# A running sum kept in HBM: ScalarE copies product blocks out of PSUM, an accumulating DMA adds them

## The chip, the cores and the metric

The kernel runs on one core of one Trainium2 chip. The core has TensorE (PE, with PEld for its weight loads), VectorE (DVE), ScalarE (ACT), GpSimd (POOL) and SyncE (SP), which work through queues of their own and wait for each other by semaphores. Tiles lie in SBUF or, as results of matmuls, in PSUM banks of 128 x 512 fp32; DMA engines move data between SBUF and HBM. The metric is the device time of one execution in microseconds, the median of the runs.

## The reference

One decoder layer for 1024 tokens of 1024 features, in fp32:

```python
x = LN1(ALPHA * x + 0.5 * swiglu(x, w_gate1, w_up1, w_down1))
x = LN2(ALPHA * x + mixer(x))
x = LN3(ALPHA * x + 0.5 * swiglu(x, w_gate2, w_up2, w_down2))
def swiglu(x, w_gate, w_up, w_down):
    return (silu(x @ w_gate) * (x @ w_up)) @ w_down
```

`D_FF` is 2816. The mixer (gated delta rule and gated linear attention) isn't touched by the change.

## The kernel before

*Tiles.* The tokens are 8 blocks of 128, in two halves of four. The features of a feed-forward layer are 22 blocks of 128. Every factor of a product is split into two parts hi and lo (`split`: ScalarE casts hi, VectorE subtracts to get lo), and a product is three matmuls. The layer's running sum is `acc`, eight SBUF tiles of 128 tokens x 1024, kept divided by ALPHA.

*A feature block.* `hidden` loads `w_gate` and `w_up` (each as two halves of 256 KB through the ring `wr` of 5, split into the ring `wh`/`wl` of 6), multiplies them with x (`proj`, 24 matmuls into a bank `pa`), and makes silu(gate) x up as tiles `gh`/`gl`. `down` multiplies with `w_down` (tiles `fh`/`fl`): for each token block and each half of the 1024 columns it runs `3 * len(hs)` matmuls into a bank `pd` (3 banks), and then one VectorE instruction adds the bank to `acc`:

```python
nc.vector.scalar_tensor_tensor(acc, p, scale / ALPHA, acc, ALU.mult, ALU.add, ...)
```

*Phases.* `run` has three parts. `ffn_groups(1, ...)` takes blocks 0 to 11 of the first layer, in six groups of two, each for all tokens: two `hidden` with both halves of the tokens, then 16 product blocks of six matmuls (8 token blocks x 2 column halves). `middle` does the rest of that layer for one half of the tokens at a time, the mixer, and the first 8 blocks of the second layer. `ffn_groups(2, ...)` takes blocks 8 to 17 in five groups of two, and then, as `last`, blocks 18 to 21 for each half together with the closing layer norm.

*What sets the order.* The code is written out in order, and a scheduler puts it into the queues. Each engine works in the order of its queue. SP issues all DMAs of the kernel before; a DMA that has to wait for a buffer holds up those behind it on SP. A ring's tile is written again only when the last reader of its earlier content is done. At the start, `acc` first serves as staging room for x transposed; `load_acc` then loads x into it.

Of the kernel before, what the change touches and what calls it, by code (L numbers as in the profile page):

```python
# [10 lines left out]
F32 = mybir.dt.float32  # L11
# [3 lines left out]
ALU = mybir.AluOpType  # L15
# [12 lines left out]
ALPHA = 2.0 ** 0.25  # L28
# the rows that the layer norms get here are the reference's over ALPHA
LN_EPS = 1e-5 / ALPHA ** 2  # L30
# [11 lines left out]
BANKS = {"pa": 2, "pd": 3, "pm": 3}  # L42
BUFS = {"w": 6, "h": 3, "xf": 3, "wr": 5, "f": 4, "g": 6, "raw": 1, "q": 1, "k": 2, "v": 1, "tt": 1, "z": 1, "on": 2, "am": 1, "pt": 1, "qd": 1, "vb": 1,
        "v0": 1, "v1": 1, "kd": 1, "mi": 1, "ui": 1, "wi": 2}
# [37 lines left out]
class Layer:  # L82
    def __init__(self, tc, ctx, a):
        self.tc, self.nc, self.a = tc, tc.nc, a
        pool = lambda name, bufs, **kw: ctx.enter_context(tc.tile_pool(name=name, bufs=bufs, **kw))
        self.cp = pool("cp", 1)
        self.xp = pool("xp", 1)
        self.wp = pool("wp", 1)
        self.sp = pool("sp", 1)
        self.ps = pool("ps", 1, space=PSUM)  # L90
        self.n = 0
        self.xh = [[None] * KB, [None] * KB]
        self.xl = [[None] * KB, [None] * KB]
        self.acc = [None] * KB
        self.mv = [None] * KB
        self.centred = {}

# [25 lines left out]
    def weight(self, src, pool=None, tag="w"):  # L123
        """The parts hi and lo of the two halves of the columns of src, in tiles of their own."""
        out = []
        for sl in HALVES:
            raw = self.u("wr", self.wp)
            self.nc.sync.dma_start(raw[:], src[:, sl])
            hi, lo = [self.wt(pool or self.wp, [HT], tag + t, BUFS[tag], F32R) for t in "hl"]
            self.split(hi[:], lo[:], raw[:])  # L130
            out.append((hi, lo))
        return out
# [28 lines left out]
    def load_x(self, half, k):  # L161
        h, l = self.xtile(half, k)
        c = 4 * half + k // 2
        if k % 2 == 0:
            # acc serves as staging room until it is loaded itself
            self.acc[c] = self.wt(self.xp, [D], f"acc{c}", 1)
        raw = self.acc[c][:, HALVES[k % 2]]
        self.nc.sync.dma_start(raw, self.a["xT"][half, k])
        self.split(h[:], l[:], raw)

    def load_acc(self, c):
        t = self.acc[c]
        self.tc.keep_in_program_order(self.nc.sync.dma_start(t[:], self.a["x"][c]))

# [13 lines left out]

    def down(self, hs, ws, half, scale, cs=range(4), sums=None, cuts=((0, HT), (HT, D)), ahead=1):
        """acc += scale / ALPHA * sum of h w for the half's token blocks cs; sums gets the new acc's sums over the columns."""  # L190
        nc = self.nc
        n = len(hs)
        units = [(c, d, cut) for d, cut in enumerate(cuts) for c in cs]
        while units:
            # the first few units take all but the last h first, which has just been computed
            now, units = units[:ahead], units[ahead:]
            ahead = 1
            yield 3 * n * len(now)
            ps = [self.bank("pd")[:, 0:cut[1] - cut[0]] for c, d, cut in now]
            for part in (range(n - 1), range(n - 1, n)) if len(now) > 1 else (range(n),):  # L200
                for p, (c, d, cut) in zip(ps, now):
                    sl, ds = slice(c * P, (c + 1) * P), slice(cut[0] % HT, (cut[1] - 1) % HT + 1)
                    for i in part:
                        (hh, hl), (wh, wl) = hs[i], ws[i][cut[0] // HT]
                        nc.tensor.matmul(p, hh[:, sl], wh[:, ds], start=(i == 0), stop=False)  # L205
                        nc.tensor.matmul(p, hh[:, sl], wl[:, ds], start=False, stop=False)  # L206
                        nc.tensor.matmul(p, hl[:, sl], wh[:, ds], start=False, stop=(i == n - 1))  # L207
            for p, (c, d, cut) in zip(ps, now):
                acc = self.acc[4 * half + c][:, slice(*cut)]
                nc.vector.scalar_tensor_tensor(acc, p, scale / ALPHA, acc, ALU.mult, ALU.add,  # L210
                                               accum_out=None if sums is None else sums[:, d:d + 1])
# [27 lines left out]
    def ln(self, i, half):  # L239
        """Normalises the half's acc, writes the parts hi and lo of the transpose of LN(acc)."""  # L240
        nc = self.nc
# [25 lines left out]
    def out_stats(self, c, sums):  # L267
        """The rows' means and reciprocal deviations; (acc - mean) * g in two temporary tiles."""
        nc = self.nc
# [54 lines left out]
    def hidden(self, idx, f, halves, pool, tags, bufs, tanh=False):  # L324
        """silu(x w_gate) * (x w_up) of one block of features (twice that with tanh), as parts hi and lo."""
        wgu = self.a[f"gu{idx}"]
# [30 lines left out]
    def ffn(self, idx, fs, half):  # L357
        """The blocks fs of features for one half of the tokens, two at a time."""
        for n in range(0, len(fs), 2):
# [7 lines left out]
    def ffn_groups(self, idx, groups, first=False, last=()):  # L367
        """Blocks of features in groups, both halves of the tokens, while the mixer needs no room."""
        with self.tc.tile_pool(name=self.nm("fx"), bufs=1) as fx:
            for n, fs in enumerate(groups):  # L370
                hs = []
# [6 lines left out]
                if first and n == 1:  # L378
                    self.load_constants()
            if last:  # L380
                for half in range(2):
                    hs = [now(self.hidden(idx, f, (half,), fx, ("gh", "gl"), BUFS["g"])) for f in last]
                    self.downs_group(idx, last, hs, (half,), fx, end=True)

    def downs_group(self, idx, fs, hs, halves, fx, first=False, end=False):
        ws = [self.weight(self.a[f"wd{idx}"][f], *((fx, "f") if 2 * n < BUFS["f"] else ())) for n, f in enumerate(fs)]
        if first:
            for c in range(KB):
                self.load_acc(c)
        for half in halves:  # L390
            for c in range(4):
                sums = self.tiny("sums", 2) if end and c < 3 else None
                last = end and half == 1 and c == 3
                work = self.down([h[half] for h in hs], ws, half, 0.5, [c], sums,
                                 ((0, HT), (HT, HT + HT // 2), (HT + HT // 2, D)) if last else ((0, HT), (HT, D)))
                if end:
# [28 lines left out]
    def misc(self, half):  # L425
        nc = self.nc
        sm = lambda tag, w=16: self.wt(self.sp, [w], tag, 1)
        # columns 64:128 repeat 0:64 in memory; here they become the parts lo, so the sum of both halves is the product
        w = []
# [77 lines left out]
    def finish(self, ons, half, blk, wz, wcol):  # L507
        """Gates heads' normalised outputs [token, dv] and adds their share of w_out."""
        nc = self.nc
# [17 lines left out]
    def pull(self, n, skip=0):  # L527
        """Emits about n products of the work that waits, from its entry number skip on."""
        while n > 0 and len(self.urgent) + len(self.filler) > skip:
# [30 lines left out]
    def gdn(self, h, half, free):  # L560
# [49 lines left out]

        # the inverse of each B0 x B0 diagonal block of I + A, column after column from the last
        m, w = self.u("mi"), self.u("wi")
# [7 lines left out]
        for j in range(B0 - 1, 0, -1):  # L620
            # row j of each block, in all of the block's partitions
            bk = self.wt(self.sp, [NC, B0], "bk", 2)
# [13 lines left out]
        for b in LEVELS:  # L636
            # the columns of the second halves of the blocks of 2 * b
            second = lambda a: a.rearrange("p (n t w) -> p n t w", t=2, w=b)[:, :, 1, :]
# [17 lines left out]
        for b in (32, 64):  # L656
            # block by block, as the halves of the blocks begin at partitions that the engines can start at
            blk = [(c, j, slice(j, j + b), slice(j + b, j + 2 * b)) for j in range(0, P, 2 * b) for c in C2]
# [4 lines left out]
            pw, m = self.bank("pm"), self.u("mi")  # L663
            # over all rows of the block, as the others are zero: all products that write a bank start at the same row
            for c, j, f, s in blk:
# [44 lines left out]
    def values(self, ws, half):  # L710
        """The pair's values with the tokens on the partitions: both weights have the columns of both heads, for half of the rows."""
        out = []
# [46 lines left out]
    def gla(self, p, half, free):  # L759
# [41 lines left out]
        for i, hb in enumerate(GLEVELS):  # L801
# [7 lines left out]
            nc.scalar.activation(e[:], e[:], AF.Exp, scale=N)  # L809
            # the rows of the second halves are masked below, so that any finite numbers serve there  # L810
            if i:
# [168 lines left out]
```

## Time and profile before

| | |
|---|---|
| median of 3 runs | 2101.03 us (2100.22 to 2102.66) |
| span of the profiled execution | 2097.4 us |
| what lies around the span, by the median | 3.6 us |
| DVE L210, the addition to `acc` | 433 instructions, 293.8 us |
| all weights and x read from HBM | 157.06 MB |

The page gives no time of its own for the profiled execution beside the span; the runs stand 2.8 to 5.3 us above it. From the trace the parts of the program lie so: first phase to 402 us, `middle` to some 1634 us, second phase to some 1960 us, then `last`. Busy times of PE are of pipelined matmuls and overlap; counts of matmuls in a stretch tell the pace better than their mean duration. In a row of a group, the part behind the bar is busy time and mean duration of one, and then the engine's idle time before these instructions with what ended it.

### The profile page before, as it was taken

To read this page: it belongs to the slowest core of one execution; us is meant where nothing else is said; L and a number is where in the kernel's file an instruction comes from. 1 tells how busy PE (TensorE), PEld (TensorE's weight loads), DVE (VectorE), ACT (ScalarE), POOL (GpSimd) and SP (SyncE) were. 2 spreads that over 40 slices of the span, in tenths; PEclk is the share of its full clock that TensorE was granted. 3 is DMA by queue.
4 is the path that set the end of the run, shared out by engine and by line. 5 is a ranking of instruction groups with operands and counts; after the bars stand their busy time and mean duration, and the time that the engine had idled before them with its cause. 6 is when DMAs were issued, how large, how long until landed. Compare 5 with 4: busy or idle time off the path is not lost.

```text
span 2097.4 us, 27456 instructions
## 1 busy us (share of the span) xinstructions
PE 2067.7 (99%) x10292; PEld 1695.0 (81%) x10292; DVE 1284.9 (61%) x2793; ACT 697.2 (33%) x1395; POOL 54.6 (3%) x87
## 2 busy tenths in 40 slices
PE   9999999999999999999999999999999999999998
PEld 7888888888887787788788777888788888888887
DVE  4434333454678888768899887778755333333456
ACT  5211121123254444434464443343422211112232
POOL 0000000000000000000101000001000000000000
PEclk9999999999999999999999999999999999999999
DMA  8111111122222212222131222122323211111232
GB/s 288 49 55 48 43 55 46 46 97 99 89 93 86 71 56 79 70 69 91 66 111 66 71 76 66 66 71 71 121 96 105 80 46 46 51 40 61 76 106 85
DMA packets 87109, 163.03 MB, mean 78 GB/s; under 512 B 10048, under 2 KB 10560, under 8 KB 86976
## 3 DMA queue, kind: packets, MB, share of 16 engines
q1 hardware_dynamic: 86976, 161.29, 22.9%
q8 instruction: 80, 1.31, 0.3%
q14 instruction: 53, 0.43, 0.1%
HBM read 157.06 MB, written 4.19 MB: 77 GB/s over the span
## 4 chain that ended last, share of the span: by engine, by line
PE 87%; DVE 8%; ACT 2%; issue 2%; POOL 1%; DMA 1%; SPq 0%; DVEq 0%; ACTq 0%; POOLq 0%
PE pa L183 17%; PE pa L184 17%; PE pa L186 17%; PE pd L205 8%; PE pd L206 8%; PE pd L207 8%; PE pm L824 1%; PE pm L422 1%; DVE wl L121 1%; DVE acc L210 1%; DVE acc L264 1%; PE pa L724 1%; DVE xl L121 1%; PE pa L725 1%; PE pa L723 1%
## 5 line engine op out<-in xcount | busy, mean ns | idle before, releaser
L183 PE MATMUL pa<-xh,wh 128*128 128x512 f32 x1808 | 716.6, 397 | 8.7 <-ACT xh L120 5.1
L184 PE MATMUL pa<-xl,wh 128*128 128x512 f32 x1808 | 708.7, 392 | 0.1
L186 PE MATMUL pa<-xh,wl 128*128 128x512 f32 x1792 | 704.3, 393 | 0.0
L121 DVE TENSOR_TENSOR wl<-wr,wh 128x512 fp32r<-128x512 f32 (+1 forms) x489 | 334.1, 686 | 350.9 <-ACT wh L120 340.9
L120 ACT CAST wh<-wr 128x512 fp32r<-128x512 f32 (+1 forms) x489 | 302.6, 621 | 709.5 <-PE pa L184 482.9
L183 PEld LDWEIGHTS pa<-xh,wh 128*128 128x128 f32 x1808 | 340.5, 188 | 80.0 <-ACT xh L120 5.9
L184 PEld LDWEIGHTS pa<-xl,wh 128*128 128x128 f32 x1808 | 340.3, 188 | 68.0 <-DVE xl L121 1.8
L186 PEld LDWEIGHTS pa<-xh,wl 128*128 128x128 f32 x1792 | 337.2, 188 | 67.9
L210 DVE SCALAR_TENSOR_TENSOR acc<-pd,acc 128x512 f32<-128x512 f32 x433 | 293.8, 687 | 125.4 <-PE pd L207 122.0
L205 PE MATMUL pd<-wh,hh 128*128 128x512 f32 x416 | 165.4, 404 | 2.2 <-ACT xf L254 1.4
L206 PE MATMUL pd<-wl,hh 128*128 128x512 f32 x416 | 164.2, 396 | 0.1
L207 PE MATMUL pd<-wh,hl 128*128 128x512 f32 x416 | 162.1, 395 | 0.0
L319 DVE TENSOR_TENSOR xf<-xf,pa 128x512 f32<-128x512 f32 x88 | 60.4, 686 | 165.8 <-PE pa L186 165.8
L206 PE MATMUL pd<-fl,gh 128*128 128x512 f32 (+1 forms) x386 | 150.0, 389 | 0.0
L205 PE MATMUL pd<-fh,gh 128*128 128x512 f32 (+1 forms) x386 | 150.0, 389 | 0.0
L207 PE MATMUL pd<-fh,gl 128*128 128x512 f32 (+1 forms) x386 | 149.8, 388 | 0.0
L205 PEld LDWEIGHTS pd<-wh,hh 128*128 128x128 f32 x416 | 78.1, 188 | 24.2 <-ACT hh L120 5.1
L120 ACT CAST fh<-wr 128x512 fp32r<-128x512 f32 x52 | 32.2, 622 | 195.4 <-PE pd L207 165.6
L207 PEld LDWEIGHTS pd<-wh,hl 128*128 128x128 f32 x416 | 78.1, 188 | 17.7 <-DVE hl L121 2.9
L206 PEld LDWEIGHTS pd<-wl,hh 128*128 128x128 f32 x416 | 78.3, 188 | 13.9 <-DVE wl L121 0.8
L205 PEld LDWEIGHTS pd<-fh,gh 128*128 128x128 f32 x386 | 72.5, 188 | 15.2
L207 PEld LDWEIGHTS pd<-fh,gl 128*128 128x128 f32 x386 | 72.5, 188 | 15.2
(251 smaller groups left out, 1987.5 us busy)
## 6 DMA issues: line engine op xcount, KB each, us to landing
wr<-gu SPq DMA_DIRECT2D x263, 256.0 KB, 2.5
wr<-wd SPq DMA_DIRECT2D x132, 256.0 KB, 2.6
wr<-win SPq DMA_DIRECT2D x116, 256.0 KB, 2.6
wr<-wout SPq DMA_DIRECT2D x32, 256.0 KB, 2.5
acc<-xT SPq DMA_DIRECT2D x16, 256.0 KB, 5.4
acc<-x SPq DMA_DIRECT2D x8, 512.0 KB, 8.7
out_dram<-acc SPq DMA_DIRECT2D x7, 512.0 KB, 2.6
g<-lnrow SPq DMA_DIRECT2D x9, 256.0 KB, 3.4
```

Source lines behind the costliest of these rows:

```text
L120: self.nc.scalar.copy(hi, src)
L121: self.nc.vector.tensor_tensor(lo, src, hi.bitcast(F32), ALU.subtract)
L183: nc.tensor.matmul(ps[:], hi[:, sl], xh[k][:], start=(k == 0), stop=False)
L184: nc.tensor.matmul(ps[:], hi[:, sl], xl[k][:], start=False, stop=(lo is None and k == KB - 1))
L186: nc.tensor.matmul(ps[:], lo[:, sl], xh[k][:], start=False, stop=(k == KB - 1))
L205: nc.tensor.matmul(p, hh[:, sl], wh[:, ds], start=(i == 0), stop=False)
L206: nc.tensor.matmul(p, hh[:, sl], wl[:, ds], start=False, stop=False)
L207: nc.tensor.matmul(p, hl[:, sl], wh[:, ds], start=False, stop=(i == n - 1))
L210: nc.vector.scalar_tensor_tensor(acc, p, scale / ALPHA, acc, ALU.mult, ALU.add, accum_out=None if sums is None else sums[:, d:d + 1])
L264: nc.vector.tensor_tensor(acc, acc, g[:], ALU.mult)
L319: self.nc.vector.tensor_tensor(s[:], s[:], ps[:], ALU.mult)
L422: self.nc.tensor.transpose(self.chunk(ps, c), s, self.ident)
```

## The change

In the groups of the two phases (not in `last`, and not in `middle`) a product block goes another way. ScalarE copies and scales it out of PSUM into a new ring `ev` of four SBUF tiles, and a DMA issued by GpSimd adds the tile to `accd`, a copy of the running sum in HBM. At the start of the first phase x goes from HBM straight into `accd`; at the start of the second, `acc` is stored there; at the end of each phase `accd` is loaded into `acc`. To make room for `ev`, the ring of `gh`/`gl` has 4 tiles in place of 6.

```diff
-BUFS = {"w": 6, "h": 3, "xf": 3, "wr": 5, "f": 4, "g": 6, ...
+BUFS = {"ev": 4, "w": 6, "h": 3, "xf": 3, "wr": 5, "f": 4, "g": 4, ...
...
+        self.dp = pool("dp", 1, space=bass.MemoryType.DRAM)
...
+        self.accd = [None] * KB
...
-    def load_acc(self, c):
-        t = self.acc[c]
-        self.tc.keep_in_program_order(self.nc.sync.dma_start(t[:], self.a["x"][c]))
...
+    def spill(self, c, src):
+        self.accd[c] = self.dp.tile([P, D], F32, name=self.nm("accd"), tag=f"accd{c}", bufs=1)
+        self.nc.sync.dma_start(self.accd[c][:], src)
+
+    def unspill(self, c):
+        self.nc.sync.dma_start(self.acc[c][:], self.accd[c][:])
+
+    def add_out(self, p, c, cut, scale):
+        t = self.u("ev", self.fx)
+        self.nc.scalar.activation(t[:], p, AF.Copy, scale=scale / ALPHA)
+        self.nc.gpsimd.dma_start(self.accd[c][:, slice(*cut)], t[:], accum_op=ALU.add)
...
             for p, (c, d, cut) in zip(ps, now):
+                if out:
+                    self.add_out(p, 4 * half + c, cut, scale)
+                    continue
                 acc = self.acc[4 * half + c][:, slice(*cut)]
...
         with self.tc.tile_pool(name=self.nm("fx"), bufs=1) as fx:
+            self.fx = fx
+            if not first:
+                for c in range(KB):
+                    self.spill(c, self.acc[c][:])
             for n, fs in enumerate(groups):
...
+            for c in range(KB):
+                self.unspill(c)
             if last:
...
         if first:
             for c in range(KB):
-                self.load_acc(c)
+                self.spill(c, self.a["x"][c])
...
-                                 ((0, HT), (HT, HT + HT // 2), (HT + HT // 2, D)) if last else ((0, HT), (HT, D)))
+                                 ((0, HT), (HT, HT + HT // 2), (HT + HT // 2, D)) if last else ((0, HT), (HT, D)), out=not end)
```

TensorE's queue has the same instructions in the same order. The other queues change as follows.

VectorE before, at the end of the first phase's third group: the additions of the last product blocks to `acc`, with the subtractions for the next `w_down` (`fl`) between them.

```order
L210 SCALAR_TENSOR_TENSOR acc5_42_166<-pd_254_1427,acc5_42_166 128x512
L210 SCALAR_TENSOR_TENSOR acc5_42_166<-pd_255_1435,acc5_42_166 128x512
L210 SCALAR_TENSOR_TENSOR acc6_47_177<-pd_256_1443,acc6_47_177 128x512
L210 SCALAR_TENSOR_TENSOR acc6_47_177<-pd_257_1451,acc6_47_177 128x512
L121 TENSOR_TENSOR fl_306_1754<-wr_304_1751,fh_305_1753 128x512
L210 SCALAR_TENSOR_TENSOR acc7_52_188<-pd_258_1459,acc7_52_188 128x512
L121 TENSOR_TENSOR fl_309_1760<-wr_307_1757,fh_308_1759 128x512
L210 SCALAR_TENSOR_TENSOR acc7_52_188<-pd_259_1467,acc7_52_188 128x512
```

In the changed kernel VectorE has no additions there; ScalarE has the copies at the same place of the program, between the casts for the next `w_down` (`fh`):

```order
L197 ACTIVATE ev_305_1528<-pd_304_1521 128x512
L197 ACTIVATE ev_307_1538<-pd_306_1531 128x512
L197 ACTIVATE ev_309_1548<-pd_308_1541 128x512
L197 ACTIVATE ev_311_1558<-pd_310_1551 128x512
L122 CAST fh_361_1859<-wr_360_1857 128x512
L197 ACTIVATE ev_313_1568<-pd_312_1561 128x512
L122 CAST fh_364_1865<-wr_363_1863 128x512
L122 CAST fh_367_1871<-wr_366_1869 128x512
L197 ACTIVATE ev_315_1578<-pd_314_1571 128x512
L122 CAST fh_370_1877<-wr_369_1875 128x512
L328 ACTIVATE xf_323_1618<-pa_322_1593 128x512
```

The silu of the next group (`xf`) stands behind the copies now, and behind the casts as before. GpSimd's queue, which had nothing in the phases, has the adds; here those of the same copies and the first of the next group:

```order
L198 DMA accd_104_485<-ev_305_1528 128x512
L198 DMA accd_104_485<-ev_307_1538 128x512
L198 DMA accd_105_487<-ev_309_1548 128x512
L198 DMA accd_105_487<-ev_311_1558 128x512
L198 DMA accd_106_489<-ev_313_1568 128x512
L198 DMA accd_106_489<-ev_315_1578 128x512
L198 DMA accd_99_475<-ev_373_1888 128x512
L198 DMA accd_99_475<-ev_375_1898 128x512
```

Two adds in a row go to the two column halves of one token block, and neither waits for the other; the next add to the same half of a block comes a group later.

SP's queue around the end of the first phase, before: `gu1` are `w_gate` and `w_up`, `wd1` is `w_down` of the first two feature blocks of `middle`, and then follow the weights of the next two.

```order
L128 DMA wr_501_2885<-gu1 128x512
L128 DMA wr_504_2891<-gu1 128x512
L128 DMA wr_510_2927<-wd1 128x512
L128 DMA wr_513_2933<-wd1 128x512
L128 DMA wr_516_2939<-wd1 128x512
L128 DMA wr_519_2945<-wd1 128x512
L128 DMA wr_530_3015<-gu1 128x512
L128 DMA wr_533_3021<-gu1 128x512
```

And in the changed kernel:

```order
L130 DMA wr_614_3137<-wd1 128x512
L130 DMA wr_617_3143<-wd1 128x512
L130 DMA wr_620_3149<-wd1 128x512
L193 DMA acc0_9_93<-accd_99_475 128x1024
L193 DMA acc1_16_112<-accd_100_477 128x1024
L193 DMA acc2_21_123<-accd_101_479 128x1024
L193 DMA acc3_26_134<-accd_102_481 128x1024
L193 DMA acc4_37_157<-accd_103_483 128x1024
L193 DMA acc5_42_168<-accd_104_485 128x1024
L193 DMA acc6_47_179<-accd_105_487 128x1024
L193 DMA acc7_52_190<-accd_106_489 128x1024
L130 DMA wr_623_3155<-wd1 128x512
```

The eight loads of `acc`, each of which waits for the last adds to its token block, stand ahead of the last half of `w_down`. At the start of the second phase, four of the stores of `acc` stand ahead of three halves of the first group's `w_down` (`wd2`):

```order
L130 DMA wr_3279_15127<-wd2 128x512
L190 DMA accd_3231_14843<-acc4_37_157 128x1024
L190 DMA accd_3232_14845<-acc5_42_168 128x1024
L190 DMA accd_3233_14847<-acc6_47_179 128x1024
L190 DMA accd_3234_14849<-acc7_52_190 128x1024
L130 DMA wr_3282_15133<-wd2 128x512
L130 DMA wr_3285_15139<-wd2 128x512
L130 DMA wr_3288_15145<-wd2 128x512
```

They wait for VectorE's last additions to these tiles. The other four are issued earlier.

More of the change, by code (lines that the diff above doesn't have):

```diff
@@ L42 @@
 BANKS = {"pa": 2, "pd": 3, "pm": 3}
-BUFS = {"w": 6, "h": 3, "xf": 3, "wr": 5, "f": 4, "g": 6, "raw": 1, "q": 1, "k": 2, "v": 1, "tt": 1, "z": 1, "on": 2, "am": 1, "pt": 1, "qd": 1, "vb": 1,
+BUFS = {"ev": 4, "w": 6, "h": 3, "xf": 3, "wr": 5, "f": 4, "g": 4, "raw": 1, "q": 1, "k": 2, "v": 1, "tt": 1, "z": 1, "on": 2, "am": 1, "pt": 1, "qd": 1, "vb": 1,
         "v0": 1, "v1": 1, "kd": 1, "mi": 1, "ui": 1, "wi": 2}
@@ L187, in proj, with down @@
         return ps
-    def down(self, hs, ws, half, scale, cs=range(4), sums=None, cuts=((0, HT), (HT, D)), ahead=1):
+    def spill(self, c, src):
[7 more added lines that the diff above has]
+        self.nc.gpsimd.dma_start(self.accd[c][:, slice(*cut)], t[:], accum_op=ALU.add)
+    def down(self, hs, ws, half, scale, cs=range(4), sums=None, cuts=((0, HT), (HT, D)), ahead=1, out=False):
         nc = self.nc
```

## The prediction

> **What bounds the kernel now.** First the page's busy times, then the same in stretches of time (columns: stretch, its length, then for PE, PEld, DVE, ACT, POOL the busy us and in brackets the instructions, then the granted clock, the DMA share and GB/s).
>
> ```profile
> span 2097.4 us, 27456 instructions
> PE 2067.7 (99%) x10292; PEld 1695.0 (81%) x10292; DVE 1284.9 (61%) x2793; ACT 697.2 (33%) x1395; POOL 54.6 (3%) x87
> 100.00:200.00 100.00, 100.00 (x442) 82.73 (x441) 37.83 (x56) 17.55 (x29) 0.00 (x0) 1.00 0.13 45
> 300.00:400.00 100.00, 100.00 (x443) 82.73 (x442) 39.78 (x59) 16.29 (x27) 0.00 (x0) 1.00 0.13 43
> 1700.00:1800.00 100.00, 100.00 (x442) 82.76 (x441) 31.09 (x47) 19.33 (x32) 0.00 (x0) 1.00 0.15 52
> 1800.00:1900.00 100.00, 100.00 (x442) 82.70 (x441) 41.68 (x62) 17.73 (x29) 0.00 (x0) 1.00 0.14 48
> ```
>
> TensorE bounds it. In the two phases that the change touches PE is busy for all of every stretch, at 442 matmuls in 100 us, 0.226 us each, whatever VectorE does beside it, and the granted clock is 1.00. GpSimd does nothing there. So the change, which leaves TensorE's instructions and their order alone, has nothing to win in these phases; it can only make TensorE wait.
>
> The timeline of VectorE at the end of the first phase, with a row on the next block (start, duration, idle before), and the page's group:
>
> ```profile
> 385.91 0.69 DVE L210 SCALAR_TENSOR_TENSOR acc<-pd,acc 128x512 f32<-128x512 f32 x1 [0.67 <-PE pd L207]
> 387.27 0.69 DVE L210 SCALAR_TENSOR_TENSOR acc<-pd,acc 128x512 f32<-128x512 f32 x1 [0.67 <-PE pd L207]
> 400.88 0.69 DVE L210 SCALAR_TENSOR_TENSOR acc<-pd,acc 128x512 f32<-128x512 f32 x1 [0.68 <-PE pd L207]
> 425.32 1.29 DVE L210 SCALAR_TENSOR_TENSOR acc<-pd,acc 128x512 f32<-128x512 f32 x2 [0.59 <-PE pd L207]
> L210 DVE SCALAR_TENSOR_TENSOR acc<-pd,acc 128x512 f32<-128x512 f32 x433 | 293.8, 687 | 125.4 <-PE pd L207 122.0
> ```
>
> A product block (six matmuls) is ready every **1.36 us**, and VectorE waits for it each time (0.67 us idle). A group of two feature blocks makes 16 of them, 21.8 us, and then TensorE has 2 x 4 projections of 24 matmuls, 43.4 us, without a block. There are 6 such groups in the first phase and 5 in the second, 176 blocks.
>
> **The change, part by part.**
>
> *VectorE loses* 176 additions of 0.687 us, 121 us. It was waiting for TensorE in front of them, so this is worth **0**.
>
> *ScalarE gains* 176 copies out of PSUM. The nearest rows:
>
> ```profile
> L314 ACT ACTIVATE xf<-pa 128x512 f32<-128x512 f32 x52 | 31.0, 595 | 69.8 <-PE pa L186 69.8
> L120 ACT CAST gh<-xf 128x512 fp32r<-128x512 f32 x52 | 32.3, 622 | 126.3 <-DVE xf L319 126.3
> ```
>
> 0.6 us each, one every 1.36 us, beside an engine that is busy 16 to 20 us in 100: hidden behind the matmuls, 0, and a bank is free 0.1 us sooner than before. The smaller ring of h tiles (4 for 6) costs 0 too: a group needs 4, and the next group's first cast into one waits, as the second row shows, for a VectorE product, which comes after projections that TensorE does after the group's last block.
>
> *The adds themselves* are what counts. Copy 5 needs the tile that add 1 reads, copy 9 that of add 5, copy 13 that of add 9, and block 16 needs the PSUM bank that copy 13 empties. Block 1 is out and copied at 1.36 + 0.6 = 1.96 us, TensorE begins block 16 at 15 x 1.36 = 20.4 us. I write L for the time from a finished copy to the landing of its add, and X for the time between two landings when the DMA engines (or GpSimd's issuing) are the limit; a copy and its hand-over take 0.7. Then TensorE waits, in each group, for the larger of
> - 3 (L + 0.7) + 1.96 - 20.4, above zero from **L = 5.4 us**, and
> - 1.96 + L + 8 X + 0.7 - 20.4 = 8 X + L - 17.7, above zero (at L = 3.4) from **X = 1.79 us**.
>
> So 4 tiles and 3 banks let the adds run a third slower than the blocks at no cost, since the 43.4 us behind each group empties the queue. No accumulating DMA and no DMA of GpSimd stands in this trace. Nearest rows (to landing; queue sums; stretches with the DMA engines full; one small instruction of GpSimd):
>
> ```profile
> wr<-gu SPq DMA_DIRECT2D x263, 256.0 KB, 2.5
> acc<-xT SPq DMA_DIRECT2D x16, 256.0 KB, 5.4
> out_dram<-acc SPq DMA_DIRECT2D x7, 512.0 KB, 2.6
> out_dram<-acc SPq DMA_DIRECT2D x2, 256.0 KB, 2.0
> q1 hardware_dynamic: 86976, 161.29, 22.9%
> 10.00:15.00 5.00, 5.00 (x21) 4.04 (x21) 3.95 (x6) 4.76 (x7) 0.00 (x0) 1.00 1.06 398
> 249.50:271.50 22.00, 22.00 (x99) 18.19 (x98) 13.18 (x21) 2.10 (x4) 0.00 (x0) 1.00 0.08 24
> L852 POOL TENSOR_TENSOR sso<-sso,mhalf 128x2 f32<-128x2 f32 x16 | 13.2, 828 | 229.8 <-DVE sso L851 229.8
> ```
>
> **X.** 161.29 MB kept 16 engines busy for 22.9% of 2097.4 us, 480 us: 0.78 us for a copy of 256 KB (0.66 us at the 398 GB/s of the full stretch). An add reads 256 KB from SBUF and 256 KB from HBM and writes 256 KB. Below it costs as one copy, 0.78; above as three passes in a row, 2.34. A copy's read and write lie side by side within its 0.78, so the add has one read more than a copy: I take 2 x 0.78 = **1.56 us**, or 1.70 beside the 8% that other transfers take in such a stretch (249.5 to 271.5). Issuing is in X as well: the smallest work of GpSimd takes 0.83 us, so at least that, and no row bounds it above.
> The Trainium skill, "Collectives: The Full Stack" (section "The bandwidth ceiling: the fold count and why AG ≠ RS ≠ AR"), says that a reducing transfer is limited by its two source reads while the addition in the DMA engine costs nothing. By that rule, twice the row's 0.78, X is an estimated 1.56 us and the sum 0; at the upper bound of the rows, three passes, it is 71 us. No run here shows yet which.
>
> **L.** Below, 2.0, as a store of 256 KB. Above, a load and a store after each other, 4.5, or a landing while the engines are full, 5.4 (second row). A store of 512 KB reads as many bytes as an add, 2.6; with 0.8 for GpSimd's issuing I take **3.4 us**. Both values stay under their limits: 8 x 1.70 + 3.4 - 17.7 = -0.7. Sum of this part **0**; at X = 2.34 and L = 5.4 it is 6.4 us a group, 11 x 6.4 = 71 us.
>
> *The transfers at the ends of the phases* go through SP's queue, in order with the weights. Rows of SP's queue:
>
> ```profile
> 24.41 5.57 SPq L173 DMA_DIRECT2D acc<-x  x8
> 404.81 0.33 SPq L128 DMA_DIRECT2D wr<-wd  x1
> 407.53 0.33 SPq L128 DMA_DIRECT2D wr<-gu  x1
> 1627.71 6.55 SPq L128 DMA_DIRECT2D wr<-wd  x4
> 40.00:45.00 5.00, 5.00 (x24) 4.14 (x23) 2.59 (x4) 2.77 (x5) 0.00 (x0) 1.00 0.56 185
> L210 DVE SCALAR_TENSOR_TENSOR acc<-pd,acc x433: 407/691/706, 53.7 to 2090.1; 128x512 f32<-128x512 f32 x144, 128x256 f32<-128x256 f32 x1
> ```
>
> - Start: x goes from HBM to HBM instead of into acc. Before, the eight loads were issued from 24.4 us and the engines were relieved at some 42 us; at twice that, 18 us become 36 and end at 60, while the first token block is added to at 54.4 and the eighth 19 us later. The first row's copy is issued ahead of three weights. 0.
> - End of phase 1: SP waits for the last add before it can issue a w_down half that was issued at 404.81 before. The last block is out at 400.9; 0.6 + 3.4 later is 404.9, and TensorE needs that weight after four projections, at some 424. 0, with 15 us to spare for the loads of acc in front of it (4 MB, of which 3.5 go earlier).
> - Start of phase 2: four stores of acc wait for the last additions of the mixer's phase and hold three w_down halves issued before at 1627.7 to 1634. These are needed after the first group's projections, 43 us later. 0.
> - End of phase 2: as in phase 1, the weight behind the loads is the sixth in line of the next projections, 27 us on. 0.
>
> **The sum** is 0 on the profiled execution's span of 2097.4 us. The median of the runs is 2101.03, 3.6 us more, which lies around the span and is not touched. Forecast **2101 us**.
>
> **The rivals.**
>
> *A, slower: the adds are transferred too slowly.* Place: the ring of four tiles, then the PSUM banks. It decides from X = 1.79. At X = 2.0 and L = 3.4 the wait is 1.7 us a group, 19 us, 2120; at three passes and the full-engine landing 2172. For it: nothing in the trace measures an addition in flight, and the margin is 0.1 us of 1.79. Against it: copies reach 398 GB/s, twice 0.66 is 1.31. Chance 0.25.
>
> *B, slower: GpSimd's issuing or the landing is long.* It decides at L = 5.4. At L = 6.5 the wait is 3.2 us a group, 35 us, 2136; at L = 8 it is 7.7, 85 us, 2186. For it: 5.4 is a landing that the trace shows, though with loads that fill the engines. Against it: 2.0 to 2.6 elsewhere. Chance 0.15.
> The Trainium skill, "SBUF — State Buffer" (section "SBUF: two separate sides"), speaks against DMAs of GpSimd: while VectorE runs an instruction that takes both its SBUF ports, GpSimd cannot write descriptors and the DMA engines idle. If VectorE's splits of 0.69 us do so, L grows by up to 0.69 us for some adds, to 4.1. By that rule B's margin shrinks from 2.0 to 1.3 us, and its chance would be 0.20; no run here shows it.
>
> *C, slower: SP is held at a phase end.* If the last adds come 15 us late, a w_down half is late by what exceeds the margin, 5 to 10 us, 2106 to 2111. It needs A or B to be strong. Chance 0.07.
>
> *D, faster: relief of VectorE.* All of PE's idle time is 2097.4 - 2067.7 = 29.7 us, none of it in the phases' stretches. A few us could come only at the start or the ends. Chance 0.03.
>
> **How the numbers follow.** Forecast 0.50. About 0.2% (4.2 us) is what a measurement of this kernel can tell from no change. Of A 0.02 and of C 0.01 stay below that: same 0.53, slower 0.44, faster 0.03. Range: from 2097, a small gain, to 2172, A's upper end. Left out are half of B (0.08), an X above three passes (0.05) and a larger gain (0.02), 0.15 in all.
>
> **What would show it.** In the new trace PE stays at 442 matmuls in the same stretches, ScalarE's copies start every 1.36 us and wait for PE, and POOL's issues are 1.36 apart. Landings of over 5.4 us, or copies that wait for a DMA from the fifth on with PE waiting for ScalarE near the end of each group, mean A or B; A when the DMA share is near 1 in the groups, B when it is not. SP idle at 405 us followed by a PE wait on a weight means C. The forecast is wrong if an add takes the DMA engines over 1.79 us or GpSimd over that to issue.

## The result, and the profile after

The changed kernel takes 2121.74 us (median of 4 runs, 2119.35 to 2124.54), the kernel before 2100.62 (4 runs, 2099.03 to 2102.66): a ratio of **1.0103** [1.0088, 1.0117], slower by 21 us. The profiled span is 2120.9 us, 23.5 more than before. (Every run for which a span is listed took 1.8 us more than its span, so the profiled execution before was one of about 2099.2 us, below its median, and the spans differ by more than the medians do. The 3.6 us given around the span before hold this spread as well.)

From the page of the changed kernel: span, busy times, the queue of GpSimd's DMAs, the median landing of the adds, and the groups of the adds and of ScalarE's copies:

```profile
span 2120.9 us, 27982 instructions
PE 2079.5 (98%) x10292; PEld 1696.4 (80%) x10292; DVE 1166.7 (55%) x2617; ACT 796.7 (38%) x1571; POOL 206.9 (10%) x263
q0 software_dynamic: 25344, 46.15, 14.5%
accd<-ev POOLq DMA_DIRECT2D x176, 256.0 KB, 5.8
L198 POOL DMA_DIRECT2D accd<-ev x176 | 152.3, 875 | 765.0 <-ACT ev L197 764.5
L197 ACT ACTIVATE ev<-pd 128x512 f32<-128x512 f32 x176 | 105.3, 598 | 158.3 <-DMA accd<-ev 109.6
```

VectorE has lost 118 us and ScalarE has copies of 0.6 us, as costed. GpSimd issues an add in 0.88 us, less than the 1.36 between blocks, and sat idle 765 us until a copy came, so issuing is no limit. The new thing is in the last row: ScalarE waits 109.6 us **for adds to land**. They land after 5.8 us in the median, above the 5.4 at which the ring of four tiles begins to cost, and they took the 16 DMA engines 0.145 x 2120.9 / 176 = 1.75 us each.

Stretches of the changed kernel: the projections ahead of the second group, that group, a stretch beside the quoted one of before, the end of the first phase, and the end of the second (columns as in the prediction):

```profile
98.00:119.50 21.50, 21.50 (x96) 17.81 (x95) 5.18 (x9) 5.13 (x10) 0.00 (x0) 1.00 0.18 55
119.50:145.50 26.00, 25.31 (x110) 20.28 (x109) 3.50 (x6) 11.84 (x21) 12.94 (x15) 1.00 0.97 147
300.00:400.00 100.00, 98.30 (x432) 80.68 (x431) 19.01 (x28) 30.78 (x52) 20.09 (x24) 1.00 0.54 103
400.00:425.00 25.00, 23.21 (x99) 17.89 (x98) 4.66 (x7) 8.86 (x15) 8.61 (x12) 1.00 1.04 262
1900.00:2000.00 100.00, 95.33 (x406) 76.75 (x405) 19.01 (x28) 30.81 (x52) 20.71 (x24) 0.98 0.70 155
```

TensorE keeps its full pace while projections run and loses it inside the groups: 432 matmuls in the stretch that had 443. The DMA share is 0.18 ahead of the group and 0.97 in it, at only 147 GB/s, where loads reached 398 at a full share. The place can be seen in ScalarE's timeline of the second group (start, duration, idle before and what ended it), with a view of the group's adds and, behind it, PE's waits for copies in the whole execution:

```profile
124.94 0.60 ACT L197 ACTIVATE ev<-pd 128x512 f32<-128x512 f32 x1 [0.76 <-PE pd L218]
126.34 0.60 ACT L197 ACTIVATE ev<-pd 128x512 f32<-128x512 f32 x1 [0.81 <-PE pd L218]
127.71 0.60 ACT L197 ACTIVATE ev<-pd 128x512 f32<-128x512 f32 x1 [0.77 <-PE pd L218]
130.51 0.60 ACT L197 ACTIVATE ev<-pd 128x512 f32<-128x512 f32 x1 [2.20 <-DMA accd<-ev]
131.79 0.60 ACT L197 ACTIVATE ev<-pd 128x512 f32<-128x512 f32 x1 [0.69 <-PE pd L218]
133.99 0.60 ACT L197 ACTIVATE ev<-pd 128x512 f32<-128x512 f32 x1 [1.59 <-DMA accd<-ev]
...
143.51 0.60 ACT L197 ACTIVATE ev<-pd 128x512 f32<-128x512 f32 x1 [0.71 <-DMA accd<-ev]
```

```profile
DMA to landing us min/median/max: 3.7/5.9/7.6
```

```profile
PE pd L216 <- ACT ev L197: 11.7, 17, 2.0
```

The first three rows are copies four to six: they wait for TensorE and start about 1.4 us apart. The seventh waits for the third add, and from there on most wait for an add. The first landing of the group takes 3.7 us from its issue, the later ones up to 7.6: adds come every 1.36 us and take longer than that, so a queue builds.

The waits of 11.7 us are half of the 23.5. The other half shows as *busy* time of PE (2067.7 before, 2079.5 now): matmuls are drawn for 0.39 us while the next one starts after 0.23, so a short delay disappears in the overlap, and stretches at half clock (last section) count as busy. So I compared the start of every matmul with the same matmul's start before (us lost; ordinary groups are the first five of phase 1 and the first four of phase 2):

| profiled execution | start | nine ordinary groups | the two last groups | middle | behind phase 2 | all |
|---|---|---|---|---|---|---|
| changed kernel | 0.9 | 0.3 to 2.1, sum 10.2 | 3.7 + 6.4 | 1.1 | 1.0 | 23.4 |
| the same again (e12) | 0.9 | 0.4 to 2.8, sum 11.3 | 3.2 + 5.0 | 2.2 | 0.0 | 22.5 |

Two effects of about equal size: some 1.1 us in every ordinary group, and more in the last group of each phase. The projections between the groups lose nothing. For the last groups, SP's queue at the end of the first phase:

```profile
393.60 28.88 SPq L193 DMA_DIRECT2D acc<-accd  x8
```

SP begins to issue the loads of `acc` at 393.6 us, when GpSimd has issued five of the group's sixteen adds; each load waits for the last adds to its token block. They are 8 x 512 KB, and they share the DMA engines with the adds (share 1.04 in the stretch from 400 to 425).

### The profile page after: what moved, and what is told of

Same layout as the page of the kernel before. It is cut to its first block, busy times and chain, and to the rows that moved or that the text cites. A ratio compares the mean times of both kernels' runs of the same rounds, so it can differ in the third digit from the quotient of the medians.

```text
span 2120.9 us, 27982 instructions
## 1 busy us (share of the span) xinstructions
PE 2079.5 (98%) x10292; PEld 1696.4 (80%) x10292; DVE 1166.7 (55%) x2617; ACT 796.7 (38%) x1571; POOL 206.9 (10%) x263
## 3 DMA queue, kind: packets, MB, share of 16 engines
q0 software_dynamic: 25344, 46.15, 14.5%
## 4 chain that ended last, share of the span: by engine, by line
PE 57%; issue 24%; DVE 8%; POOL 7%; ACT 2%; DMA 2%; POOLq 0%; SPq 0%; DVEq 0%; ACTq 0%
PE pa L181 11%; PE pa L182 11%; PE pa L184 11%; POOL accd L198 6%; PE pd L216 5%; PE pd L217 5%; PE pd L218 5%; PE pm L844 1%; DMA accd<-ev 1%; PE pm L442 1%; DVE wl L123 1%; DVE acc L224 1%; DVE acc L278 1%; PE pa L744 1%; DVE xl L123 1%
## 5 line engine op out<-in xcount | busy, mean ns | idle before, releaser
L198 POOL DMA_DIRECT2D accd<-ev x176 | 152.3, 875 | 765.0 <-ACT ev L197 764.5
L224 DVE SCALAR_TENSOR_TENSOR acc<-pd,acc 128x512 f32<-128x512 f32 (+1 forms) x257 | 172.2, 684 | 34.3 <-PE pd L218 32.6
L123 DVE TENSOR_TENSOR fl<-wr,fh 128x512 fp32r<-128x512 f32 x52 | 35.0, 691 | 252.0 <-ACT fh L122 252.0
L216 PE MATMUL pd<-fh,gh 128*128 128x512 f32 (+1 forms) x386 | 153.4, 398 | 12.0 <-ACT ev L197 11.7
L197 ACT ACTIVATE ev<-pd 128x512 f32<-128x512 f32 x176 | 105.3, 598 | 158.3 <-DMA accd<-ev 109.6
```

What stands on the lines that cost most here:

```text
L123: self.nc.vector.tensor_tensor(lo, src, hi.bitcast(F32), ALU.subtract)
L197: self.nc.scalar.activation(t[:], p, AF.Copy, scale=scale / ALPHA)
L198: self.nc.gpsimd.dma_start(self.accd[c][:, slice(*cut)], t[:], accum_op=ALU.add)
```

## The experiments

Theories: **X**, the adds are transferred too slowly (rival A); **L**, a single landing is long (rival B); and, for the last groups, the loads beside the last adds. Losses by place are from the comparison of matmul starts.

### e1: a plain store

```diff
-        self.nc.gpsimd.dma_start(self.accd[c][:, slice(*cut)], t[:], accum_op=ALU.add)
+        self.nc.gpsimd.dma_start(self.accd[c][:, slice(*cut)], t[:])
```

> The same 176 DMAs from GpSimd, but plain stores into the HBM sum; the additions of the two phases' product blocks are left out, so the running sum keeps only the last block of each place. Theory Q (the adds fill the DMA engines: 1.75 us of all 16 each, so the queue grows and the ring of four ev tiles runs dry): a store takes about 0.8 us, no copy waits for a landing, the waits of PE L216 for ACT L197 (11.7 us) vanish, 2100 to 2104 us. Theory I (GpSimd's issuing, 0.86 us each, limits): the issues are as long as before, so the waits stay, 2117 to 2122. Theory R (a landing takes a fixed 5.8 us on GpSimd's path, whatever the engines do): landings stay near 5.8 and the waits stay at 8 to 12 us.

Measured: 2104.42 us, ratio 1.0015 [1.0005, 1.0024]. Its page's queue and landing, and its stretch of the second group:

```profile
q0 software_dynamic: 14080, 46.15, 5.7%
accd<-ev POOLq DMA_DIRECT2D x176, 256.0 KB, 2.3
119.50:144.50 25.00, 25.00 (x112) 20.65 (x111) 3.97 (x6) 12.89 (x22) 8.63 (x16) 1.00 0.53 190
```

No group loses anything, the last ones included. A store takes 0.057 x 2103.0 / 176 = 0.68 us of the engines and lands in 2.3; the engines are half busy. So it is the addition in the DMA, and neither copies, tiles nor the loads at the ends by themselves. (A store is also issued faster, 0.54 us for 0.88; that issuing isn't the cause follows from e3, where adds are issued in 0.88 us and nothing is lost.) The profiled execution is 5.6 us longer than the one before, and none of it lies in the groups: 2.1 at the start, 1.6 in `middle` and 1.9 behind the last matmul.

### e3, e6, e9, e11: a deeper ring

The change had already taken two tiles from the ring `g` to make room for `ev`, but `acc` lies idle in these phases. The copies go into halves of its tiles: 16, 6 or 5 of them in turn (shown for 16).

```diff
-        t = self.u("ev", self.fx)
-        self.nc.scalar.activation(t[:], p, AF.Copy, scale=scale / ALPHA)
+        i, self.nev = self.nev, self.nev + 1
+        t = self.acc[i % 16 // 2][:, HALVES[i % 2]]
+        self.nc.scalar.activation(t, p, AF.Copy, scale=scale / ALPHA)
```

> The copies go into the idle acc tiles (16 half tiles as the ring) instead of the four ev tiles. Theory Q or R: no copy waits for a landing within a group, landings get longer (6 to 14 us at the end of a group), PE does not wait for ScalarE, 2100 to 2105. If the loss comes from elsewhere (weights that land late beside the adds, SP at the ends), 5 to 15 us of it stay: 2106 to 2116.

> Six half tiles of the idle acc as the ring. By the formula copy 13 then waits for add 7 and that for copy 7 and add 1: 2 (L + 0.7) + 1.96 - 20.4 is above zero from L = 8.5 us. Theory Q: landings reach 7 to 8 in an ordinary group, no loss there; in the last group of each phase, beside the loads of acc, they reach 9 to 12 and 0 to 5 us are lost. 2101 to 2109. If ordinary groups still lose 0.5 us or more each, the ring isn't what limits.

> Five half tiles of the idle acc as the ring. By the formula copy 13 waits for add 8, copy 8 for add 3, and copy 3 ends at 4.7 us: 2 (L + 0.7) + 4.7 - 20.4 is above zero from L = 7.2 us. Theory Q: adds in the middle of an ordinary group land in 5 to 7 us, so an ordinary group loses 0 to 0.4 us; the last groups, beside the loads of acc, 0.5 to 3 us each. 2101 to 2108.

> The ring of five lost nothing in any group in its profiled execution, 2101.1 us, yet the median of its runs was 2105.2. Theory S: the rest is single stretches of about 3.4 us at half clock, each worth some 1.6 us, and the groups lose 0 in every execution; then this execution, at about 2105, shows 0.0 us in all eleven groups and two or three such stretches elsewhere. Theory T: the groups do lose in the usual execution, because five tiles stand close to their limit (two times landing + 0.7, plus 4.68, against 20.4, so 7.2 us of landing against 6.0 measured); then this execution shows PE waits for the copies of 0.2 to 0.5 us a group, 2 to 5 us. If it comes out near 2101 again it tells nothing new.

| tiles | median, us | ratio | lost in the groups |
|---|---|---|---|
| 16 (e3) | 2102.41 | 1.0008 [0.9998, 1.0018] | 0.0 |
| 6 (e6) | 2101.65 | 1.0005 [0.9996, 1.0015] | 0.0 |
| 5 (e9) | 2105.24 | 1.0021 [1.0012, 1.003] | 0.0 |
| 5, again (e11) | 2103.66, one execution | | 0.1 |

The queue of adds in e3's profile, its stretch of the second group, and the landings of that group's adds:

```profile
q0 software_dynamic: 25344, 46.15, 13.7%
119.50:144.50 25.00, 25.00 (x111) 20.66 (x111) 2.46 (x4) 10.90 (x19) 13.84 (x16) 1.00 1.04 172
```

```profile
DMA to landing us min/median/max: 3.6/5.5/9.3
```

With room the queue builds freely, from 3.6 us for the first add to 9.3 at its longest, and costs nothing, since the 43 us of projections empty it. The engines are full for the whole group (1.04). This is theory X measured undisturbed: 0.137 x 2099.8 / 176 = 1.63 us of the engines for an add, and 26.3 us between the landings of the first and the sixteenth add of that group, 1.75 each. One tile more than four removes the loss in the groups. (In these kernels the loads of `acc` also wait for the copies that lie in its tiles, and in the profile of six tiles SP reached them four blocks before the end; so they don't tell how much of the last groups' loss is whose.)

Five tiles were slower in the median, though neither of their two profiles shows it in a group: of the 4.4 us in e11's, 2.5 lie in `middle`, 1.2 behind phase 2 and 0.6 at the start. That speaks against theory T. Of theory S's two or three stretches at half clock there is one, 3.4 us in `middle`, worth at most 1.7 of the 4.4. Both profiled executions were below the median of 2105.24, so where an execution at the median loses its time is not shown.

### e4: three tiles

```diff
-BUFS = {"ev": 4, ...
+BUFS = {"ev": 3, ...
```

> Three ev tiles instead of four. Theory Q: with three adds in flight the queue is shorter, landings fall to 4.5 to 5.2 us, and the engines still work nearly all of a group: a group loses 2 to 4 us, 2130 to 2150. Theory R (landing fixed at 5.8): copies come in threes every 6.5 us, 4 x 6.5 + 2.0 - 20.4 = 7.6 us a group, 2180 to 2190.

Measured: 2165.64 us, ratio 1.0308 [1.0293, 1.0324], between the two expectations. Landings of the first twelve adds of the second group, and the waits of PE:

```profile
DMA to landing us min/median/max: 3.6/4.8/5.4
```

```profile
PE pd L216 <- ACT ev L197: 35.1, 46, 3.1
```

Ordinary groups lose 4.2 to 5.8 us, 4.7 in the mean, the last ones 7.7 and 11.8. Here at most three adds are under way and the landing itself rules. With three tiles copy 13 hangs on adds 10, 7, 4 and 1: 4 (L + 0.7) + 1.96 - 20.4, where L is 4.8 and 0.3 more for GpSimd to begin (121.46 to 121.75 us in the profile of the change: a copy's end, its add's issue), 5.1. That gives 4.8 us; the formula holds. The expected landings (4.5 to 5.2 us) were right; by the formula they give 3.6 to 6.4 us a group, so the expected 2 to 4 were too small. (In both last groups the granted clock also was 0.50 for a while, 3.4 and 10.2 us, so not all of the 7.7 and 11.8 are waits for copies.)

### e5: half the width

```diff
-        self.nc.gpsimd.dma_start(self.accd[c][:, slice(*cut)], t[:], accum_op=ALU.add)
+        self.nc.gpsimd.dma_start(self.accd[c][:, cut[0]:cut[0] + HT // 2], t[:, 0:HT // 2], accum_op=ALU.add)
```

> Each add takes 256 of its block's 512 columns (128 KB instead of 256 KB); the additions to the other columns are left out. Ring of four as in the change. Theory Q (the add's time on the DMA engines, 1.75 us against a block every 1.36 us, makes the queue): an add takes 0.9 us, no queue builds up, landings fall to the 3.0 to 3.7 us of the first adds of a group, no PE wait in the groups, 2101 to 2105. Theory R2 (an add's read-modify-write has a latency of some 5 us of its own): landings stay at 5 or more, and some 8 to 15 us of loss stay.

Measured: 2105.65 us, ratio 1.0028 [1.0019, 1.0037]. Queue and landing of the page, and the waits of PE:

```profile
q0 software_dynamic: 25344, 23.08, 9.1%
accd<-ev POOLq DMA_DIRECT2D x176, 128.0 KB, 3.1
```

```profile
PE pd L216 <- ACT ev L197: 3.7, 2, 2.0
```

An add of 128 KB takes 0.091 x 2106.6 / 176 = 1.09 us, less than 1.36, so no queue builds: the ordinary groups lose 0.0. The last groups still lose 2.0 and 3.8, which the expectation did not have. That separates the second effect: the loads of `acc` are enough to slow adds that keep up everywhere else.

### e2: the loads of acc behind the last adds

```diff
-        self.nc.sync.dma_start(self.acc[c][:], self.accd[c][:])
+        self.tc.keep_in_program_order(self.nc.sync.dma_start(self.acc[c][:], self.accd[c][:]))
...
-            for c in range(KB):
+            for c in reversed(range(KB)):
                 self.unspill(c)
```

> The eight loads of acc at the end of each phase are issued from the last token block to the first and kept in that order on SP, so none starts before the last add has landed. Theory Q with contention: in the trace the last groups of the phases lose 3.7 and 6.4 us, the other nine 1.1 us each; without loads beside the last adds they lose 0.5 to 2 us each, so 6 to 9 us are won, 2112 to 2116. If the last groups are slow for another reason, 2119 to 2124. If SP's weights come late behind 4 MB of loads, PE waits on a weight after the phase and the gain is smaller.

Measured: 2121.81 us, ratio 1.0102 [1.0087, 1.0117]: no gain. SP's queue at the end of the first phase, a piece of the chain that ended last, and a wait of PE that the change did not have:

```profile
418.50 3.73 SPq L193 DMA_DIRECT2D acc<-accd  x8
422.33 0.76 SPq L130 DMA_DIRECT2D wr<-wd  x1
```

```profile
423.52 9.50 DMA wr<-gu
```

```profile
PE pd L216 <- ACT hh L122: 2.8, 1, 2.8
```

The loads now begin at 418.5 instead of 393.6, and the last groups fall from 3.7 and 6.4 us (e12: 3.2 and 5.0) to 1.4 and 1.3, what an ordinary group loses, and their first nine landings are 1.85 and 1.79 us apart instead of 2.14 and 2.40: the loads had cost the rest, some 5 to 7 us. But it is given back in `middle`, which loses 9.3 us: the weights of the next projections now stand behind 4 MB of loads, one lands 9.5 us after its issue, and TensorE waits 2.8 us for a factor that needs it; the rest of the 9.3 lies in stretches at half clock, 13.7 us in all. The profiled execution, 2125.12 us, was the slowest of four, so the 9.3 is more than a usual execution loses there. This is rival C's place, and it came only where the loads were held on purpose.

### e7: the small ring of g alone

The kernel before with `"g": 4` for 6.

> The kernel before with the smaller ring of h tiles alone (4 for 6). All theories: no wait of PE or ScalarE for it, 2099 to 2103, the same as before. If it costs, PE waits on gh at the starts of the down products and 1 to 5 us of the loss are its.

Measured: 2100.61 us, ratio 1.0001 [0.9991, 1.001], nothing lost in any group. The ring of four costs nothing.

### e8, e10: one add for both halves

Both column halves are copied into `acc[c]`, and one DMA adds 128 x 1024.

```diff
-        t = self.u("ev", self.fx)
-        self.nc.scalar.activation(t[:], p, AF.Copy, scale=scale / ALPHA)
-        self.nc.gpsimd.dma_start(self.accd[c][:, slice(*cut)], t[:], accum_op=ALU.add)
+        t = self.acc[c][:, slice(*cut)]
+        self.nc.scalar.activation(t, p, AF.Copy, scale=scale / ALPHA)
+        if cut[1] == D:
+            self.nc.gpsimd.dma_start(self.accd[c][:], self.acc[c][:], accum_op=ALU.add)
```

> Both halves of a token block are copied into its acc tile and one DMA adds 128 x 1024 (rows of 4 KB, 512 KB) in place of two of 256 KB; ring of eight such tiles. If an add's time on the DMA engines goes by bytes: 3.5 us for each of 88 adds, 14 to 15% of the span on GpSimd's queue as before. If it goes by rows or packets: 1.8 to 2.6 us each, 7 to 11%. Time 2100 to 2105 in both cases, since the ring doesn't bind.

> The kernel of e8 again, timed: adds of 128 x 1024 from the idle acc tiles. Theory Q: nothing of the loss stays, and nothing is won over the kernel before, since TensorE was never waiting for VectorE's additions: ratio 0.999 to 1.002. If VectorE's 121 us less were worth something, it would show here as under 0.998.

One execution took 2099.82 us (span 2097.8); timed, 2103.30 us, ratio 1.0012 [1.0003, 1.0021]. The queue and the landing in e8's profile:

```profile
q0 software_dynamic: 12672, 46.14, 12.1%
accd<-acc POOLq DMA_DIRECT2D x88, 512.0 KB, 5.3
```

An add of 512 KB takes 0.121 x 2097.8 / 88 = 2.88 us, against 2 x 1.63 for two of 256 KB: better by a ninth, so cost goes neither by bytes alone nor by rows alone. No group loses anything, VectorE is relieved of 119 us, and the time is still not below the kernel before. No version found beats it.

### e12: the change once more

> The change once more, for a second profiled execution. If the losses come from the ring and from the loads of acc, as the theory says, they stand at the same places with the same sizes: 0.3 to 2.1 us in each of the nine ordinary groups, about 10 us in all, and 3 to 7 us in each of the two last groups, about 10 us in all; only the half-clock stretches and the start may differ. If the ordinary groups come out below 5 us in all, the first profile was not typical and the account of 10 + 10 falls. 2119 to 2125 us.

2121.84 us; its row stands in the table of the result. Same places, sizes within 2 us: 11.3 in the ordinary groups, 8.1 in the last ones.

## Why the prediction was wrong

**The bound.** Right. TensorE bounds the phases; 118 us of VectorE's work went away and e8, which keeps that relief without a wait in the groups, is no faster than before. Rival D had nothing.

**Copies, issuing, the ring of g.** Right at 0: copies took 0.6 us, issuing 0.88 (the nearest row had been 0.83), and e7 lost nothing.

**The adds, the step that failed.** The prediction wrote the wait of a group as the larger of two terms, and got 0 from L = 3.4 and X = 1.70 (1.56 alone), 0.7 us below the limit of the second. The place was right. **L was too short, which used up nearly all of the 0.7, and the two limits were worked out apart, as if X did not depend on the ring.** An add alone takes 3.7 us from its issue, 4.0 from the copy's end, which lowers the limit for X from 1.79 to (17.7 - 4.0) / 8 = 1.71. X itself had been sized well, as the deeper rings show. Spacing of the first nine landings of a group, mean of the nine ordinary groups in one profile each:

| tiles | 16 (e3) | 6 (e6) | 5 (e9) | 4 (the change) | 3 (e4) |
|---|---|---|---|---|---|
| us | 1.66 | 1.68 | 1.67 | 1.79 | 2.01 |

With the 1.67 of the deeper rings and L = 4.1, the mean of these groups in the change, 8 X + L - 17.7 is -0.2, about no loss. With four tiles the same adds land 1.79 us apart, above the limit. Matched stretches of the second group (21 us from 2 us behind the first issue; the change, then e3) show the engines busy alike and moving less:

```profile
123.70:144.70 21.00, 20.31 (x89) 16.12 (x88) 0.75 (x2) 8.75 (x16) 10.93 (x14) 1.00 1.07 152
122.20:143.20 21.00, 21.00 (x95) 17.34 (x94) 1.98 (x3) 9.73 (x17) 12.32 (x15) 1.00 1.09 173
```

So with fewer adds under way each one keeps the engines longer; why, is not shown. With the landings of single adds put into the formula, for all groups of the change:

| group | L | X | 8 X + L - 17.7 | lost |
|---|---|---|---|---|
| 1 | 5.0 | 1.64 | 0.4 | 0.7 |
| 2 | 4.0 | 1.84 | 1.0 | 1.3 |
| 3 | 4.0 | 1.73 | 0.2 | 0.6 |
| 4 | 4.0 | 1.81 | 0.8 | 1.2 |
| 5 | 4.4 | 1.82 | 1.3 | 1.6 |
| 6 (last of phase 1) | 4.0 | 2.14 | 3.4 | 3.7 |
| 7 | 4.0 | 1.94 | 1.8 | 2.1 |
| 8 | 4.0 | 1.87 | 1.2 | 1.6 |
| 9 | 3.9 | 1.72 | -0.1 | 0.3 |
| 10 | 4.0 | 1.74 | 0.3 | 0.7 |
| 11 (last of phase 2) | 4.0 | 2.40 | 5.5 | 6.4 |

The formula is 0.3 to 0.4 us short in ten groups, 0.9 in the last, and follows the sizes. With X read from the same trace this only shows that the chain (ring, copy 13, bank) is the right one; it does not say beforehand what X a ring of four will have. For other rings the factor 8 becomes 9, 7 or 6 (three, five, six tiles), so at L = 4.0 five tiles stand up to X = 1.96 and six up to 2.28: no loss in ordinary groups, as measured.

X had been taken as twice a copy's 0.78. The Trainium skill, "Collectives: The Full Stack" (section "The bandwidth ceiling: the fold count and why AG ≠ RS ≠ AR"), gives the two source reads of a ReduceScatter as its limit, and by that rule X was an estimated 1.56. Measured are 1.63 to 1.75 us of all engines, so the rule is near but not enough here; beside the 0.68 of the plain store the add is dearer by a factor of 2.4, not 2.

**The transfers at the ends of the phases, the second step that failed.** They were costed at 0 by asking when SP can issue the weight behind the loads. That part was right (rival C appeared only in e2). Not asked was what the loads do to the adds that are still under way: they share the DMA engines, X in the last groups rose to 2.14 and 2.40, and the two lost 10.1 us in place of two ordinary 1.1. For the ends of the phases the prediction asked whom SP holds up, and not who shares the engines.

**The sum.** 10.2 (ordinary groups) + 10.1 (last groups) = 20.3 of 23.4 us. The other 3 are not the adds: 0.9 at the start, where kernels with the same start lost 0.0 to 2.1, and two stretches of 3.4 us at half clock, in `middle` and behind phase 2 (last section). The first stands in profiles without any loss in the groups too.

**The rivals.** A had the place (ring, then banks), the signs named for it (share near 1 in the groups, copies that wait for a DMA) and the size: its 2120 at X = 2.0, L = 3.4 was 19 us, from 11 groups alike. In fact nine were milder and two dearer, so that its total comes so near is partly luck. B's long landing was there, 5.8, but as the queue of A: a lone add takes 3.7. That GpSimd is held up beside VectorE's splits, B's second ground, is not seen in its issuing: 0.86 us in the median, the longest of 176 took 1.56.

## What to carry to other kernels

Before a running sum is handed to accumulating DMAs, compare the engine time of one add with the interval at which blocks come. If it is longer, a queue builds, and the number of tiles must cover it until the next pause, with room to spare, since with a smaller ring the landings also came further apart (1.66 to 1.68 us with five tiles and more, 1.79 with four, 2.01 with three). Here 4 tiles lost 21 us, while 6 (with the later loads that came with them) lost nothing measurable. A bulk load that follows a burst of adds takes part in the same engines: cost it by what it does to the transfers in flight, not only by what stands behind it in its queue. And where a sum of 0 hangs on a margin of a tenth of a microsecond in a value that no trace shows, a right formula still decides little.

## What the runs showed of the hardware

- An fp32 add of 256 KB (rows of 2 KB, SBUF to HBM) by an accumulating DMA kept all 16 engines busy for 1.63 to 1.75 us, the store of the same tile 0.68. Adds of 128 KB took 1.09 and of 512 KB (rows of 4 KB) 2.88: by an estimate from these three sizes about 0.5 us for each add of 128 rows and 0.6 for each 128 KB.
- GpSimd took 0.88 us to issue an add (mean of the 176 in its row) and 0.54 to issue the store (8.63 us for 16 in e1's stretch), with 144 packets for an add in its queue and 80 for a store (25344 and 14080 over 176).
- TensorE's granted clock fell to half for 3.4 us at single places. In the changed kernel's profile there are two, each behind a pause in which PE was busy for 1.3 to 1.4 of 3.4 us (rows 1 and 3, before the fall; rows 2 and 4, the fall):

```profile
1047.00:1050.40 3.40, 1.27 (x4) 0.78 (x5) 3.31 (x7) 2.90 (x6) 0.00 (x0) 1.00 0.41 133
1050.40:1053.80 3.40, 3.40 (x9) 2.63 (x8) 2.38 (x5) 0.62 (x1) 0.00 (x0) 0.50 0.57 178
1975.40:1978.80 3.40, 1.43 (x7) 0.87 (x6) 0.00 (x0) 0.60 (x1) 0.65 (x2) 1.00 1.10 262
1978.80:1982.20 3.40, 3.40 (x10) 2.67 (x9) 0.00 (x0) 1.19 (x2) 1.42 (x3) 0.51 1.09 275
```

- Such a pause alone does not decide it. The one in `middle` stands in the kernel before too, and there the clock stayed:

```profile
1036.80:1040.20 3.40, 0.98 (x4) 0.49 (x3) 3.31 (x7) 3.30 (x7) 0.00 (x0) 1.00 0.33 114
1040.20:1043.60 3.40, 3.31 (x14) 2.73 (x15) 3.24 (x7) 0.62 (x1) 0.00 (x0) 1.00 0.67 190
```

It fell there in the profiles of the change, e1 to e5, e9, e11 and e12, and not in those of the kernel before, e6, e7, e8 and e10. What decides between them is open. A fall is worth up to 1.7 us, part of what kernels without any loss in the groups still differ by.
